# Projecting the gate's two halves in one 512-wide unit at the end of a phase, and reordering the phase

## The chip, the cores and the metric

The kernel runs on one core of a Trainium2 chip. A core has a matrix engine (TensorE, in the profile PE for matmuls and PEld for its weight loads), a vector engine (VectorE, DVE), a scalar engine (ScalarE, ACT), a general engine (GpSimd, POOL) and a queue engine that issues most transfers (SyncE, SP). Each works through its own list of instructions in order and waits on semaphores for the others. Operands lie in SBUF, matmul results in eight PSUM banks of 128 x 512 floats, weights and inputs in HBM. The metric is the device time of one execution in microseconds (us).

## The reference

One layer of a streaming encoder is computed for 1024 prompt rows and 32 sample rows, width 1024, all in float32. What matters here is the first half of the layer:

```python
mod = jax.nn.silu(c) @ w_ada + b_ada
sh1, sc1, g1, sh2, sc2, g2 = jnp.split(mod[:, None, :], 6, axis=-1)
h = x * (1 + sc1) + sh1
mq, mk, mv, mo, mi, mf, fq, fk, fv, ff, gu, gv = jnp.split(h @ w_in, split_at, axis=-1)
hm, (C1, n1, m1) = _mlstm(...)           # 4 heads; mo is its output gate
hf = _fox_prompt(...)                    # 8 heads of causal attention with a decay
vn = _layer_norm(gv, gmlp_ln_g, gmlp_ln_b)
hg = _spatial_gate(gu, vn, gmlp_ws, gmlp_bs)   # gu * (lower-triangular 128x128 mix of vn + bias)
mix = jnp.concatenate([hm, hf, hg], axis=-1) @ w_o
```

A residual, a norm, a SwiGLU feed-forward block of width 2816 and a second norm follow. `gu` and `gv` have 256 columns each; `vn` of the sample rows is an output.

## The kernel before, in words

Every product is done in float32 by parts: an operand x is split into hi (rounded to the matmul's format) and lo = x - hi, and three matmuls (hi·hi, hi·lo, lo·hi) are summed in PSUM. For a weight tile this means a load of 128 x 1024 floats (`raw`), a cast on ACT (`whi`) and a subtraction on DVE or POOL (`wlo`); `weights` does it, with three buffers of each (RAW, WB).

The program has a first phase (0 to some 350 us) and the rest (output projection, norm, feed-forward, to 1345 us). `fm_first` begins it: it makes the modulated input h1 (hi and lo) slice by slice while it projects mq and mk. Two units of 264 columns for the attention's values and gates follow.

A "tm unit" (`tm_unit`) projects rows by columns: for each of eight row tiles of 128 rows it runs 8 x 3 matmuls with the rows as the stationary operand and 256 columns of weights moving, into one of three PSUM banks named g (in the trace tm_g). The ninth tile, the 32 sample rows, uses the unsplit weights (`sample_tile`, 32 small matmuls, L416). An evacuation function then takes each tile out of PSUM.

After that the string ORDER names the units of the phase one by one: q is the projection of one attention head (512 columns, in the trace head_g), f the attention of a head over row tiles 0 to 3 (fox_s scores, fox_p probabilities, fox_t transposes, fox_pth and fox_ptl their split, fox_o the product with the values), g, a, S, s, k are parts of gates, modulation (ada) and states, v and o the mLSTM's values and output gate (tm units, stored to HBM as dmv and dmo), m0 to m3 the mLSTM chunks, which load these again (mlstm_mo), and G0 to G3 the gate's units. A p behind a name puts the weight subtraction on POOL. Units f and m are emitted with a higher priority; a scheduler of the framework turns this into one list per engine, and interleaves units. SP's transfers use eight semaphores in turn, so its list is in order too, and a load that needs an earlier store to land holds up what stands behind it.

The gate takes four tm units of 256 columns: G0 (gv, tiles 0 to 3), G1 (gu, tiles 0 to 3), G2 and G3 (the same for tiles 4 to 8). `evac_gv` reads the PSUM tile for statistics (L472, L473), the reciprocal deviation (L461 to L466, tiles brs and brt) and the normalisation (L477), then POOL multiplies and adds the norm's parameters (L478, L479) and POOL's queue stores the tile in HBM (dvn). `evac_gmlp` copies gu to SBUF, loads the normalised gv of two tiles back (gvn), runs four spatial matmuls for the pair (L848), four gating operations on DVE (L851), transposes (L856), a copy (gms, L858) and a store to dmix, from which the output projection loads its operand. The PSUM bank of the pair's first gu tile is used for the spatial product and the transposes too.

Of the kernel before, what the change touches and what calls it, by code (L numbers as in the profile page):

```python
# [69 lines left out]
class Kernel:  # L70
# [34 lines left out]
    def weights(self, src, nk, ncol, eng=None, pool=None):  # L105

        nc = self.nc
        pool, width = (pool, 1024) if pool else (self.wp, 1056)
        out = []
        step = min(nk, 1056 // ncol)  # L110
        for k0 in range(0, nk, step):
# [1 line left out]
            raw = self.t(self.wp, [P, 1056], F32, "raw", RAW)
# [1 line left out]
            hi = self.t(pool, [P, width], F32R, "whi", WB)
            lo = self.t(pool, [P, width], F32R, "wlo", WB)
            nc.scalar.copy(hi[:, :w], raw[:, :w])  # L117
            (eng or nc.vector).tensor_tensor(lo[:, :w], raw[:, :w], f(hi[:, :w]), ALU.subtract)  # L118
# [348 lines left out]

    def evac_gv(self, tt, ps, n):
        nc = self.nc
        st = self.t(self.sm, [P, 6], F32, "bst", 2)  # L470
        mv = self.t(self.sm, [P, 2], F32, "bmv", 2)
        nc.vector.bn_stats(st[:n], ps[:n, :256])  # L472
        nc.vector.bn_aggr(mv[:n], st[:n])  # L473
        r = self.t(self.sm, [P, 1], F32, "brs", 2)
        self.rstd(r[:n], mv[:n, 1:2], self.eps5[:n], self.sm, "brt")
        v = self.t(self.sm, [P, 256], F32, "traw", 2)
        nc.vector.tensor_scalar(v[:n], ps[:n, :256], mv[:n, 0:1], r[:n], ALU.subtract, ALU.mult)  # L477
        nc.gpsimd.tensor_tensor(v[:n], v[:n], self.rowp[:n, 272:528], ALU.mult)  # L478
        nc.gpsimd.tensor_tensor(v[:n], v[:n], self.rowp[:n, 528:784], ALU.add)  # L479
        self.store(self.dvn[:n, tt, :], v[:n], nc.gpsimd)  # L480
        if tt == 8:
            self.store(self.d["o_vn"], v[:n])
# [346 lines left out]
    def evac_gmlp(self, tt, ps, n, bank=None):  # L829
        nc = self.nc  # L830
        if tt < 8 and tt % 2 == 0:
            self.gu = self.t(self.sm, [P, 2, 256], F32R, "vhl", 2).bitcast(F32)
            self.gbank = ps
        if bank:
            self.gu, self.gbank = ps.unsqueeze(1), bank
        u, z = self.gu, self.gbank
        nt = 1 if tt == 8 else 2
        if tt < 8:
            nc.scalar.copy(u[:n, tt % 2], ps[:n, :256])
        if tt % 2 == 0 and tt < 8:  # L840
            return
        t0 = tt - nt + 1
        vn = self.t(self.sm, [P, 2, 256], F32, "gvn", 1)
        self.load(vn[:n, :nt], self.dvn[:n, t0:tt + 1, :])
        z = z.rearrange("p (t c) -> p t c", t=2)[:n, 2 - nt:]
        for g in range(4):
            q = slice(64 * g, 64 * g + 64)
            nc.tensor.matmul(z[:, :, q], self.wsp[:n, g, :n], vn[:n, :nt, q], start=True, stop=True)  # L848
# [1017 lines left out]
```

## Time and profile before

| | |
|---|---|
| time of 3 runs | 1343.76, 1344.62, 1345.65 us; median 1344.62 |
| span of the profiled execution | 1344.9 us |
| PE busy | 1324.0 us (98%) |
| DVE, ACT, POOL busy | 989.1, 655.8, 231.9 us |
| PE idle in 200 to 250, 250 to 300, 300 to 350 us | 1.1, 0.55, 2.1 us |
| PE idle in 88 to 200 us | 0.0 us |

A row of the timeline gives start, duration, engine, line, operation and "out<-in" with shapes; in square brackets stands the idle time of the engine ahead of it and what ended that. Matmuls are pipelined: a row's duration is longer than the distance to the next start. The view of waits sums such idle times by the waiting line and the line that released it. A row with SPq is the issue of a transfer, not its duration.

### The profile page before, as it was taken

To read this page: it belongs to the slowest core of one execution; us is meant where nothing else is said; L and a number is where in the kernel's file an instruction comes from. 1 tells how busy PE (TensorE), PEld (TensorE's weight loads), DVE (VectorE), ACT (ScalarE), POOL (GpSimd) and SP (SyncE) were. 2 spreads that over 40 slices of the span, in tenths; PEclk is the share of its full clock that TensorE was granted. 3 is DMA by queue.
4 is the path that set the end of the run, shared out by engine and by line. 5 is a ranking of instruction groups with operands and counts; after the bars stand their busy time and mean duration, and the time that the engine had idled before them with its cause. 6 is when DMAs were issued, how large, how long until landed. Compare 5 with 4: busy or idle time off the path is not lost.

```text
span 1344.9 us, 25607 instructions
## 1 busy us (share of the span) xinstructions
PE 1324.0 (98%) x9684; PEld 1208.3 (90%) x9684; DVE 989.1 (74%) x2091; ACT 655.8 (49%) x1305; POOL 231.9 (17%) x263
## 2 busy tenths in 40 slices
PE   9999999999999999999999999999999999999996
PEld 6798888888999888888888888999999999999995
DVE  5635655678779667686876776678979887988777
ACT  3413445455547545545454454435754453635355
POOL 0102100143246100000000001464610000000341
PEclk9999999999999999999999999999999999999999
DMA  9585465546557754454344332663785858554221
GB/s 362 207 299 154 150 204 186 174 131 207 181 195 257 191 136 130 117 163 126 115 121 116 110 104 82 217 175 112 205 231 154 228 148 225 139 175 131 89 79 67
DMA packets 119450, 221.73 MB, mean 165 GB/s; under 512 B 18580, under 2 KB 62768, under 8 KB 119328
## 3 DMA queue, kind: packets, MB, share of 16 engines
q1 hardware_dynamic: 112096, 207.55, 49.0%
q0 software_dynamic: 6032, 11.94, 5.2%
q8 instruction: 76, 1.25, 0.4%
q10 hardware_dynamic: 1200, 0.62, 0.2%
q14 instruction: 46, 0.38, 0.1%
HBM read 188.13 MB, written 51.85 MB: 178 GB/s over the span
## 4 chain that ended last, share of the span: by engine, by line
PE 68%; DVE 4%; DMA 1%; ACT 1%; issue 1%; DVEq 0%; ACTq 0%
PE up_g L130 6%; PE up_g L132 6%; PE up_g L131 6%; PE dn_g L130 4%; PE dn_g L132 4%; PE dn_g L131 4%; PE sup_u L132 3%; PE sup_u L131 3%; PE sup_u L130 3%; PE wo_g L131 2%; PE wo_g L132 2%; PE wo_g L130 2%; PE sup_g L132 2%; PE sup_g L131 2%; PE sup_g L130 2%; PE fox_t L943 2%
## 5 line engine op out<-in xcount | busy, mean ns | idle before, releaser
L130 PE MATMUL up_g<-tm_ah,up_whi 128*128 128x512 f32 (+1 forms) x384 | 140.0, 365 | 0.0
L131 PE MATMUL up_g<-tm_al,up_whi 128*128 128x512 f32 (+1 forms) x384 | 140.0, 365 | 0.0
L132 PE MATMUL up_g<-tm_ah,up_wlo 128*128 128x512 f32 (+1 forms) x384 | 139.7, 364 | 0.0
L1368 ACT CAST sup_whi<-sup_raw 128x1024 fp32r<-128x1024 f32 x54 | 56.1, 1048 | 89.3 <-PE dn_u L131 43.9
L130 PEld LDWEIGHTS up_g<-tm_ah,up_whi 128*128 128x128 f32 x384 | 72.3, 188 | 11.1 <-DVE tm_al L1246 0.4
L132 PEld LDWEIGHTS up_g<-tm_ah,up_wlo 128*128 128x128 f32 x384 | 72.3, 188 | 11.1
L131 PEld LDWEIGHTS up_g<-tm_al,up_whi 128*128 128x128 f32 x384 | 72.3, 188 | 10.7
L916 ACT ACTIVATE fox_p<-fox_s,fox_fmx 128x384 f32<-128x384 f32 (+2 forms) x96 | 55.2, 579 | 53.0 <-DVE fox_fmx L914 41.2
L1199 DVE SCALAR_TENSOR_TENSOR wo_z<-dn_g,start_mod,wo_z 128x512 f32<-128x512 f32 (+4 forms) x120 | 60.3, 521 | 22.6 <-PE dn_g L132 22.0
L118 DVE TENSOR_TENSOR up_wlo<-up_raw,up_whi 128x1024 fp32r<-128x1024 f32 x50 | 65.2, 1305 | 15.0 <-ACT up_whi L117 13.7
L1369 DVE TENSOR_TENSOR sup_wlo<-sup_raw,sup_whi 128x1024 fp32r<-128x1024 f32 x54 | 68.0, 1263 | 10.7 <-ACT sup_whi L1368 10.7
L117 ACT CAST up_whi<-up_raw 128x1024 fp32r<-128x1024 f32 x50 | 52.4, 1048 | 47.2 <-PE up_g L131 23.9
L130 PE MATMUL dn_g<-up_acth,dn_whi 128*128 128x512 f32 (+2 forms) x200 | 73.5, 368 | 0.8 <-DVE wo_z L1199 0.8
L132 PE MATMUL dn_g<-up_acth,dn_wlo 128*128 128x512 f32 (+2 forms) x200 | 73.3, 366 | 0.0
L131 PE MATMUL dn_g<-up_actl,dn_whi 128*128 128x512 f32 (+2 forms) x200 | 72.8, 365 | 0.0
L948 ACT CAST fox_pth<-fox_t 128x512 fp32r<-128x512 f32 (+1 forms) x80 | 41.6, 542 | 59.2 <-PE fox_t L943 57.5
L117 ACT CAST dn_whi<-dn_raw 128x1024 fp32r<-128x1024 f32 (+1 forms) x44 | 42.7, 971 | 51.7 <-PE up_g L131 16.0
L911 DVE TENSOR_REDUCE fox_fmx<-fox_s 128x1 f32<-128x384 f32 (+2 forms) x96 | 52.8, 553 | 16.3 <-PE fox_s L908 15.0
L949 DVE TENSOR_TENSOR fox_ptl<-fox_t,fox_pth 128x512 fp32r<-128x512 f32 (+1 forms) x80 | 49.9, 631 | 15.9 <-ACT fox_pth L948 15.6
L118 DVE TENSOR_TENSOR dn_wlo<-dn_raw,dn_whi 128x1024 fp32r<-128x1024 f32 (+1 forms) x44 | 49.5, 1125 | 10.4 <-ACT dn_whi L117 9.5
L402 PE MATMUL tm_g<-tm_whi,start_h1h 128*128 128x256 f32 (+1 forms) x192 | 55.3, 288 | 0.7 <-DVE tm_traw L477 0.7
L1320 POOL DMA_DIRECT2D start_dp<-w_gu x19 | 19.8, 1067 | 209.0 <-DMA start_dp<-w_gu 209.0
(684 smaller groups left out, 4799.7 us busy)
## 6 DMA issues: line engine op xcount, KB each, us to landing
up_raw<-w_gu SPq DMA_DIRECT2D x50, 512.0 KB
ada_late<-w_ada SPq DMA_DIRECT2D x28, 512.0 KB
dn_raw<-w_dn SPq DMA_DIRECT2D x28, 512.0 KB
sup_raw<-w_gu SPq DMA_DIRECT2D x20, 512.0 KB
start_dp<-w_gu SPq DMA_DIRECT2D x19, 512.0 KB
start_dp<-w_gu POOLq DMA_DIRECT2D x19, 512.0 KB, 8.0
wo_raw<-w_o SPq DMA_DIRECT2D x18, 512.0 KB
sup_raw<-start_dp SPq DMA_DIRECT2D x18, 512.0 KB
```

Of the source, the lines that this page charges most:

```text
L117: nc.scalar.copy(hi[:, :w], raw[:, :w])
L118: (eng or nc.vector).tensor_tensor(lo[:, :w], raw[:, :w], f(hi[:, :w]), ALU.subtract)
L130: nc.tensor.matmul(ps, hi, xh(k), start=start and k == 0, stop=False)
L131: nc.tensor.matmul(ps, hi, xl(k), start=False, stop=False)
L132: self.lastmm = nc.tensor.matmul(ps, lo, xh(k), start=False, stop=stop and k == n - 1)
L402: nc.tensor.matmul(ps[:, :ncol], xh, hi, start=k == 0, stop=False)
L911: nc.vector.tensor_reduce(mxs[:, x:x + 1], s[:, :w], AX.X, ALU.max, negate=True)
L916: nc.scalar.activation(pr[:, lo:hi], banks[x][:, :hi - lo], AF.Exp, bias=mxs[:, 0:1], accum_out=sums[:, x:x + 1])
L949: nc.vector.tensor_tensor(pl[:, :e], ps[:, :e], f(ph[:, :e]), ALU.subtract)
L1199: self.lastz = self.nc.vector.scalar_tensor_tensor(z[:, m, x:y], ps[:, x - a:y - a], g[i], z[:, m, x:y], ALU.mult, ALU.add)
L1368: nc.scalar.copy(h, x)
L1369: tt(l, x, f(h), ALU.subtract)
```

## The change

The four gate units become one: G projects [gv | gu], 512 columns, for all nine tiles, and stands at the end of ORDER, ahead of a last a. The other units are named in a new order; the weight subtractions of G are on DVE. `evac_gv` is gone. `evac_gmlp` now works on pairs of tiles: ACT copies an even tile and then an odd tile whole to SBUF (vhl), DVE takes statistics there, the reciprocal deviation is made once for the pair, DVE normalises each tile in SBUF, POOL multiplies and adds for both tiles at once (128 x 2 x 256), and the spatial matmuls read the result where it stands. The stores to dvn and the loads of gvn are gone. The odd tile's PSUM bank is used for the spatial product and the transposes. `weights` uses tiles of 1024 instead of 1056 columns and four buffers instead of three; the 264-wide units are loaded in 3 + 3 + 2 slices instead of 4 + 4. The first v unit is issued behind the last DVE operation of `fm_first`'s last split. The scratch area of POOL's transfers is 4096 instead of the default.

```diff
-ORDER = "q0 f0 g q1 a f1 a g S q2 f2 k1p s a q3 f3 a v q4 f4 a q5 f5 o a m0 G0 q6 f6 a m1 G1p G2p q7 m2 f7 a m3 G3"
+ORDER = "q0 q1 f0 a g a f1 q2 S k1p g q3 f2 a f3 q4 a v s f4 q5 f5 a q6 o m0 m1 a m2 f6 m3 a q7 f7 G a"
-RAW = 3
+RAW = 4
-WB = 3
+WB = 4
...
-        step = min(nk, 1056 // ncol)
-        for k0 in range(0, nk, step):
+        most = 1024 // ncol
+        for k0 in range(0, nk, most):
+            step = min(most, nk - k0)
...
             self.h1_split(k + 1, h)
+            if k == KT - 2:
+                self.lasth = [i for i in nc.cur_bb.bb.instructions if i.engine == eng.DVE][-1]
...
-        self.tm_unit(w1[0], 264, self.evac_v(0))
+        with tc.issue_after(self.lasth):
+            self.tm_unit(w1[0], 264, self.evac_v(0))
...
-                self.tm_unit(w2[2 + i % 2], 256, (self.evac_gv, self.evac_gmlp)[i % 2],
-                             range(4 * (i // 2), 4 + i // 2 * 5), eng=eng)
+                self.tm_unit(d["w_in_g"], 512, self.evac_gmlp, range(9), eng=eng)
...
-    nc = bacc.Bacc("TRN2", target_bir_lowering=False, num_devices=1)
+    nc = bacc.Bacc("TRN2", target_bir_lowering=False, num_devices=1, dynamic_dma_scratch_size=4096)
```

The evacuation of the gate (the new function up to the spatial matmuls; behind them only the tile names differ):

```python
    def evac_gmlp(self, tt, ps, n, bank=None):
        nc = self.nc
        nt = 1 if tt == 8 else 2
        i, t0 = tt % nt, tt - nt + 1
        if i == 0:
            self.gst = [self.t(self.sm, [P, 2, w], F32, x, 2) for x, w in (("bst", 6), ("bmv", 2), ("brs", 1))]
            self.gx = ps.unsqueeze(1) if bank else f(self.t(self.sm, [P, 1024], F32R, "vhl", 2)).rearrange(
                "p (t c) -> p t c", t=2)
        x, (st, mv, r) = self.gx, self.gst
        if bank is None:
            nc.scalar.copy(x[:, i], ps)
        nc.vector.bn_stats(st[:n, i], x[:n, i, :256])
        nc.vector.bn_aggr(mv[:n, i], st[:n, i])
        if i < nt - 1:
            return
        self.gbank = bank or ps
        vn, u = x[:n, :nt, :256], x[:n, :nt, 256:]
        self.rstd(r[:n, :nt], mv[:n, :nt, 1:2], self.eps5[:n], self.sm, "brt")
        for y in range(nt):
            nc.vector.tensor_scalar(vn[:, y], vn[:, y], mv[:n, y, 0:1], r[:n, y], ALU.subtract, ALU.mult)
        row = lambda o: self.rowp[:n, o:o + 256].unsqueeze(1).to_broadcast([n, nt, 256])
        nc.gpsimd.tensor_tensor(vn, vn, row(272), ALU.mult)
        nc.gpsimd.tensor_tensor(vn, vn, row(528), ALU.add)
        ...
            nc.tensor.matmul(z[:, :, q], self.wsp[:n, g, :n], vn[:, :, q], start=True, stop=True)
```

How the lists of the engines move is shown at three places. First DVE's list at the end of `fm_first`, before: the slice's modulation (ada_h) and its split (start_al, start_h1l) stand behind the subtraction of the first v unit (tm_wlo).

```order
L219 TENSOR_SCALAR start_mod_153<-ada_adam_597,start_colp_108 128x2 x2
L118 TENSOR_TENSOR tm_wlo_680<-tm_raw_677,tm_whi_679 128x1056
L243 TENSOR_SCALAR ada_h_601<-fm_x_529,start_mod_153 128x1024
L244 TENSOR_SCALAR ada_h_601<-fm_x_529,start_mod_153 128x32
L253 TENSOR_TENSOR start_al_170<-ada_h_601,start_ah_169 128x512
L253 TENSOR_TENSOR start_h1l_172<-ada_h_601,start_h1h_171 128x544
```

And now:

```order
L220 TENSOR_SCALAR start_mod_152<-ada_adam_596,start_colp_107 128x2 x2
L244 TENSOR_SCALAR ada_h_600<-fm_x_528,start_mod_152 128x1024
L245 TENSOR_SCALAR ada_h_600<-fm_x_528,start_mod_152 128x32
L254 TENSOR_TENSOR start_al_169<-ada_h_600,start_ah_168 128x512
L254 TENSOR_TENSOR start_h1l_171<-ada_h_600,start_h1h_170 128x544
L119 TENSOR_TENSOR tm_wlo_679<-tm_raw_676,tm_whi_678 128x792
L119 TENSOR_TENSOR tm_wlo_685<-tm_raw_682,tm_whi_684 128x792
```

The subtraction moved behind the whole slice.

Second, ACT's list where the output gate's first tiles (tm_traw) are copied out and chunk m0 takes the gate (mlstm_mo, loaded from HBM) through Exp, Ln, Exp; before:

```order
L452 COPY tm_traw_3037<-tm_g_3012 128x256
L916 ACTIVATE fox_p_2761,fox_fsm_2760<-fox_s_2762,fox_fmx_2759 128x512
L452 COPY tm_traw_3065<-tm_g_3040 128x256
L916 ACTIVATE fox_p_2881,fox_fsm_2880<-fox_s_2882,fox_fmx_2879 128x128
L732 ACTIVATE mlstm_mo_3266<-mlstm_mo_3266 128x256
L948 CAST fox_pth_2776<-fox_t_2771 128x512
L733 ACTIVATE mlstm_mo_3266<-mlstm_mo_3266,start_ones_36_111 128x256
L948 CAST fox_pth_2785<-fox_t_2781 128x384
```

And now:

```order
L455 COPY tm_traw_3098<-tm_g_3073 128x256
L912 ACTIVATE fox_p_2893,fox_fsm_2892<-fox_s_2894,fox_fmx_2891 128x384
L944 CAST fox_pth_2806<-fox_t_2802 128x384
L912 ACTIVATE fox_p_2904,fox_fsm_2903<-fox_s_2905,fox_fmx_2902 128x512
L719 ACTIVATE mlstm_mo_3306<-mlstm_mo_3306 128x256
L720 ACTIVATE mlstm_mo_3306<-mlstm_mo_3306,start_ones_35_110 128x256
L721 ACTIVATE mlstm_mo_3306<-mlstm_mo_3306 128x256
L958 COPY fox_fo_2815<-fox_o_2781 64x512
L455 COPY tm_traw_3126<-tm_g_3101 128x256
L944 CAST fox_pth_2919<-fox_t_2914 128x512
```

The three gate operations stand together now, and the copies of an attention result and of the second tile stand behind them, ahead of the next cast for the attention.

Third, POOL's list at the gate; before, with its own stores and weight subtractions between the norms of single tiles:

```order
L478 TENSOR_TENSOR tm_traw_3422<-tm_traw_3422,start_rowp_176 128x256
L479 TENSOR_TENSOR tm_traw_3422<-tm_traw_3422,start_rowp_176 128x256
L118 TENSOR_TENSOR tm_wlo_3745<-tm_raw_3742,tm_whi_3744 128x1024
L91 DMA start_dvn_63<-tm_traw_3422 128x256
L118 TENSOR_TENSOR tm_wlo_3751<-tm_raw_3748,tm_whi_3750 128x1024
L478 TENSOR_TENSOR tm_traw_3463<-tm_traw_3463,start_rowp_176 128x256
```

And now:

```order
L837 TENSOR_TENSOR tm_vhl_3987<-tm_vhl_3987,start_rowp_175 128x2x256
L722 TENSOR_TENSOR mlstm_mo_3645<-mlstm_mo_3645,start_rowp_175 128x256
L838 TENSOR_TENSOR tm_vhl_3987<-tm_vhl_3987,start_rowp_175 128x2x256
L837 TENSOR_TENSOR tm_vhl_4072<-tm_vhl_4072,start_rowp_175 128x2x256
L838 TENSOR_TENSOR tm_vhl_4072<-tm_vhl_4072,start_rowp_175 128x2x256
```

Stores and weight subtractions are gone from it, and each operation covers a pair of tiles; the multiplication of chunk m3's gate stands between the first pair's two.

More of the change, by code (lines that the diff above doesn't have):

```diff
@@ L107, in weights @@
         nc = self.nc
[L108 removed]
+        pool, bufs = (pool, 3) if pool else (self.wp, WB)
         out = []
[L110 to L111 removed]
+        most = 1024 // ncol
+        for k0 in range(0, nk, most):
+            step = min(most, nk - k0)
             w = step * ncol
[L113 removed]
+            raw = self.t(self.wp, [P, 1024], F32, "raw", RAW)
             self.load(raw[:, :w], src[:, k0 * ncol:k0 * ncol + w])
[L115 to L116 removed]
+            hi = self.t(pool, [P, 1024], F32R, "whi", bufs)
+            lo = self.t(pool, [P, 1024], F32R, "wlo", bufs)
             nc.scalar.copy(hi[:, :w], raw[:, :w])
@@ L310, in split @@
         def split(k):
-            hi, lo = (self.t(self.wp, [P, 1056], F32R, x, WB)[:, :2 * N] for x in ("whi", "wlo"))
+            hi, lo = (self.t(self.wp, [P, 1024], F32R, x, WB)[:, :2 * N] for x in ("whi", "wlo"))
             nc.scalar.copy(hi, raw[k])
@@ L417, in sample_tile @@
                                  start=k == KT - 1, stop=k == 0)
-        r = self.t(self.sm, [NS, 264], F32, "tmsum", 1)[:, :ncol]
+        r = self.t(self.sm, [P, 512], F32, "gms", 1)[:NS][:, :ncol]
         for q in range(4):
             nc.scalar.copy(r[:, n * q:n * q + n], ps[32 * q:32 * q + 32, :n])
-        evac(8, r, NS, *([ps] if evac == self.evac_gmlp else []))
+        evac(8, r, NS, *([ps] if ncol == 512 else []))
     def evac_v(self, half):
@@ L437, in evac @@
             nc.vector.tensor_copy(self.G[:, tt, 8 * half:8 * half + 8], gate)
-            hl = self.t(self.sm, [P, 4, 2, 64], F32R, "vhl", 2)
+            hl = self.t(self.sm, [P, 1024], F32R, "vhl", 2)[:, :512].rearrange("p (h two e) -> p h two e", h=4, two=2)
             src = raw.rearrange("p (h e) -> p h e", h=4)
@@ L447, in evac_raw, with evac @@
         nc = self.nc
-        def evac(tt, ps, n):
+        def evac(tt, ps, n, bank=None):
             if tt < 8:
@@ L466, in rstd @@
         nc.vector.scalar_tensor_tensor(out, v, 1.5, out, ALU.add, ALU.mult)
[L468 to L482, printed above, removed]
     def evac_qk(self, h, act=False):
@@ L830, in evac_gmlp @@
         nc = self.nc
-        if tt < 8 and tt % 2 == 0:
-            self.gu = self.t(self.sm, [P, 2, 256], F32R, "vhl", 2).bitcast(F32)
-            self.gbank = ps
-        if bank:
[L835 to L845, printed above, removed]
+        nt = 1 if tt == 8 else 2
+        i, t0 = tt % nt, tt - nt + 1
+        if i == 0:
+            self.gst = [self.t(self.sm, [P, 2, w], F32, x, 2) for x, w in (("bst", 6), ("bmv", 2), ("brs", 1))]
[7 more added lines that the diff above has]
+        if i < nt - 1:
+            return
+        self.gbank = bank or ps
[6 more added lines that the diff above has]
+        nc.gpsimd.tensor_tensor(vn, vn, row(528), ALU.add)
+        if bank:
+            self.store(self.d["o_vn"], vn[:, 0])
+        z = self.gbank.rearrange("p (t c) -> p t c", t=2)[:n, 2 - nt:]
         for g in range(4):
             q = slice(64 * g, 64 * g + 64)
-            nc.tensor.matmul(z[:, :, q], self.wsp[:n, g, :n], vn[:n, :nt, q], start=True, stop=True)
+            nc.tensor.matmul(z[:, :, q], self.wsp[:n, g, :n], vn[:, :, q], start=True, stop=True)
         for g in range(4):
@@ L856, in evac_gmlp @@
                 nc.tensor.transpose(ps[:, i, x, :n], u[:n, x, i * P:(i + 1) * P], self.ident[:n, :n])
-        s = self.t(self.sm, [P, 2, 2, P], F32, "gms", 1)
+        s = self.t(self.sm, [P, 512], F32, "gms", 1).rearrange("p (i t q) -> p i t q", i=2, t=2)
         nc.scalar.copy(s[:, :, :nt, :n], ps[:, :, :nt, :n])
@@ L1359, in sup @@
         ah, al = act[j] = [self.t(pool, [P, GN[1]], F32R, x, 5) for x in ("acth", "actl")]
-        raw = [self.t(self.wp, [P, 1056], F32, "raw", RAW)[:, :1024] for _ in range(2)]
+        raw = [self.t(self.wp, [P, 1024], F32, "raw", RAW)[:, :1024] for _ in range(2)]
         raw.append(self.t(self.px, [P, 544], F32, "w2", 1)[:, :512])
@@ L1370, in split @@
             return [(h[:, k * P:k * P + P], l[:, k * P:k * P + P]) for k in range(x.shape[1] // P)]
-        big = lambda x: split(*(self.t(self.wp, [P, 1056], F32R, y, WB)[:, :1024] for y in ("whi", "wlo")), x)
+        big = lambda x: split(*(self.t(self.wp, [P, 1024], F32R, y, WB)[:, :1024] for y in ("whi", "wlo")), x)
         w1 = big(raw[0])
@@ L1807, in _layout @@
     a["w_in_1"] = units(np.concatenate([mq, mk[:, :128]], axis=1), 384)[0]
-    a["w_in"] = units(np.concatenate([mv, mo, gv, gu], axis=1), 256)
+    a["w_in"] = units(np.concatenate([mv, mo], axis=1), 256)
+    a["w_in_g"] = units(np.concatenate([gv, gu], axis=1), 512)[0]
     a["w_in_f"] = units(np.concatenate([mk[:, 128:], qk], axis=1), 128)
```

5 lines of the change are left out of this document (2 added, 3 removed).

## The prediction

> **What bounds the kernel now.** I read the page's totals and clock first, then the stretches of time, then what PE waited for, then single rows of the timeline.
>
> ```profile
> span 1344.9 us, 25607 instructions
> PE 1324.0 (98%) x9684; PEld 1208.3 (90%) x9684; DVE 989.1 (74%) x2091; ACT 655.8 (49%) x1305; POOL 231.9 (17%) x263
> PEclk9999999999999999999999999999999999999999
> ```
>
> TensorE (PE) is busy 98% at full clock; the other engines matter only where it waits for them. The view by stretches says where it idles.
>
> ```profile
> core 0: us, PE busy (x) PEld busy (x) DVE busy (x) ACT busy (x) POOL busy (x), PEclk, DMA share, GB/s
> 88.00:200.00 112.00, 112.00 (x907) 99.63 (x907) 63.99 (x206) 46.52 (x111) 11.21 (x18) 1.00 0.58 184
> 200.00:250.00 50.00, 48.90 (x410) 42.77 (x410) 30.15 (x77) 27.90 (x66) 1.37 (x2) 1.00 0.58 177
> 250.00:300.00 50.00, 49.45 (x439) 45.12 (x441) 34.79 (x79) 23.47 (x56) 19.77 (x19) 1.00 0.45 144
> 300.00:350.00 50.00, 47.89 (x437) 43.68 (x426) 42.21 (x125) 26.09 (x69) 13.97 (x20) 1.00 0.58 192
> ```
>
> The change edits 50 to 350 us; there PE idles 1.1 + 0.55 + 2.1 us from 200 on, and nothing from 88 to 200. The waits of PE name the causes:
>
> ```profile
> engine line waited for: us in total, times, longest us
> PE fox_o L951 <- DVE fox_ptl L949: 1.1, 1, 1.1
> PE tm_g L416 <- DVE tm_traw L477: 1.0, 1, 1.0
> PE up_u L132 <- DVE up_wlo L118: 0.8, 1, 0.8
> PE tm_g L416 <- ACT tm_traw L434: 0.7, 1, 0.7
> PE tm_g L402 <- DVE tm_traw L477: 0.7, 1, 0.7
> PE tm_g L402 <- DVE tm_brt L464: 0.6, 1, 0.6
> PE tm_g L848 <- DMA tm_gvn<-start_dvn: 0.4, 1, 0.4
> PE fm_t L329 <- ACT start_hs L254: 0.4, 1, 0.4
> ```
>
> Four of these (L477 twice, L464, the gvn load) belong to the gate's units. All the change can win by removing waits is a few us.
>
> **The change, part by part.**
>
> *Width.* 384 matmuls of 256 columns become 192 of 512. The mean durations suggest much, the starts little:
>
> ```profile
> L402 PE MATMUL tm_g<-tm_whi,start_h1h 128*128 128x256 f32 (+1 forms) x192 | 55.3, 288 | 0.7 <-DVE tm_traw L477 0.7
> 231.33 0.28 PE L404 MATMUL tm_g<-tm_whi,start_al 128*128 128x256 f32 x1
> 232.62 0.28 PE L403 MATMUL tm_g<-tm_wlo,start_ah 128*128 128x256 f32 x1
> 274.68 0.40 PE L132 MATMUL head_g<-start_ah,tm_wlo 128*128 128x512 f32 x1
> 276.08 0.39 PE L132 MATMUL head_g<-start_ah,tm_wlo 128*128 128x512 f32 x1
> ```
>
> Between the first two starts lie 11 steps, 1.29/11 = 0.117 us each; between the last two 6 steps, 1.40/6 = 0.233. Matmuls overlap, so the step is the price: 192 x (2 x 0.1173 - 0.2333) = 0.25 us. I take -0.3 (0 to -1).
>
> *Sample tile.* Two sample tiles of 256 columns (a quarter of them per matmul) become one of 512, 32 matmuls fewer.
>
> ```profile
> 322.72 1.10 PE L416 MATMUL tm_g<-tm_raw,start_hs 128*32 128x64 f32 x64 [1.04 <-DVE tm_traw L477]
> ```
>
> One costs 1.1 us with the switch into it. If columns set its time, only the switch is saved; if the count does, all of one tile. Nearer the first, as the width showed: -0.3 (0 to -1.1).
>
> *Waits of the gate's units.* Their banks were held until DVE's normalisation (L477) had read them; now ACT copies each even tile out and frees it, and the odd tile's bank is kept for the spatial product. The four waits sum to 2.7 us; a matmul's row (0.28) lasts 0.16 longer than its step (0.117), and an idle time counts only from the row's end, so each wait costs 0.16 more: 4 x 0.16 = 0.6. So 3.3 goes (2.7 to 3.4).
>
> The new chain to the spatial product replaces it:
>
> ```profile
> 266.22 0.73 POOL L478 TENSOR_TENSOR tm_traw<-tm_traw,start_rowp 128x256 f32<-128x256 f32 x1 [4.45 <-DVE tm_bmv L473]
> 268.01 0.54 DVE L477 TENSOR_SCALAR tm_traw<-tm_g,tm_bmv,tm_brs 128x256 f32<-128x256 f32 x1
> 263.08 0.43 DVE L472 BATCH_NORM_STATS2 tm_bst<-tm_g 128x6 f32<-128x256 f32 x1
> ```
>
> Per pair: ACT copy 0.6 (estimate, from a 512-wide ACT cast in 234.99 to 235.56 below), statistics 0.6, rstd about 1.2 (two ACT, three DVE steps), two L477-like operations 1.1, two POOL operations twice as wide, so 2 x 1.46 = 2.9: 6.4 us, near 7.5 with hand-overs. By the order PE has 39 matmuls of 512 ahead of the tightest spatial product, 9.1 us, and some attention work. DVE is 84% busy here (42.21 of 50), so it may queue; I charge 0.5 (0 to +2).
>
> That POOL and DVE get in each other's way is to be seen already:
>
> ```profile
> 270.65 2.40 POOL L118 TENSOR_TENSOR tm_wlo<-tm_raw,tm_whi 128x1024 fp32r<-128x1024 f32 x1 [0.40 <-ACT tm_whi L117]
> 270.70 2.36 DVE L464 SCALAR_TENSOR_TENSOR tm_brt<-tm_bmv,start_eps,tm_brs 128x1 f32<-128x1 f32 x1 [1.60 <-ACT tm_brs L462]
> ```
>
> A one-column operation took 2.36 us because POOL began 0.05 earlier. The change drops four such POOL casts and 18 narrow operations (4 x 2.4 + 18 x 0.73 = 22.7 us) for 8 of 1.46 (11.7 us). The Trainium skill, page "SBUF — State Buffer", section "Who interferes with whom", adds a point against the change: a DVE tensor_scalar that stays in SBUF can enter a mode that shares POOL's ports, and the loser waits out the whole instruction; before, L477 read PSUM. By that rule each of the 8 new POOL operations may hold DVE, at most 11.7 us of DVE, less than the 22.7 us that could hold it before; no run here shows that mode yet.
>
> *Start.* The last input slice's operations on DVE now stand ahead of the first weight split of the v unit.
>
> ```profile
> 49.20 1.25 DVE L118 TENSOR_TENSOR tm_wlo<-tm_raw,tm_whi 128x1056 fp32r<-128x1056 f32 x1
> 50.37 0.80 DVE L243 TENSOR_SCALAR ada_h<-fm_x,start_mod 128x1024 f32<-128x1024 f32 x1
> 52.54 0.83 PE L329 MATMUL fm_t<-fm_raw,start_hs 128*32 128x384 f32 x2 [0.39 <-ACT start_hs L254]
> ```
>
> The slice comes 1.17 earlier; PE gets back its 0.4 wait and some of the slack before it: -0.7 (-0.4 to -1.2). The split, now late by some 3 us, is not needed before the v unit's first tile at 59.3.
>
> *Output-gate unit, then mLSTM chunk 0.* In the new order m0 follows o at once. The gate travels through HBM: ACT copies tile 0, SP stores it, SP waits for the landing, loads it back, and ACT, in order, stands still.
>
> ```profile
> 226.71 0.36 ACT L452 COPY tm_traw<-tm_g 128x256 f32<-128x256 f32 x1
> 227.81 0.34 SPq L91 DMA_DIRECT2D start_dmo<-tm_traw  x1
> 232.53 0.34 SPq L87 DMA_DIRECT2D mlstm_mo<-start_dmo  x1
> 234.67 0.42 ACT L732 ACTIVATE mlstm_mo<-mlstm_mo 128x256 f32<-128x256 f32 x1 [4.17 <-DMA mlstm_mo<-start_dmo]
> 234.99 0.57 ACT L948 CAST fox_pth<-fox_t 128x512 fp32r<-128x512 f32 x1
> 352.55 0.46 SPq L91 DMA_DIRECT2D start_dmix<-fox_fo  x1
> 354.86 0.33 SPq L87 DMA_DIRECT2D tm_al<-start_dmix  x1
> ```
>
> Landing took 4.7 us behind queued weight loads, 2.3 at 352.55. In the new order ACT has three mo operations (1.35), a 64x512 copy (0.6), a tile copy (0.36) and the cast (0.57) after the load, DVE the 0.63 split (its group's mean): 3.5 us. From the end of tile 0: 1.5 to the store's issue, 2.3 to 4.7 landing, 2.1 load, 3.5 = 9.4 to 11.8 us. PE has 57 narrow matmuls (6.7) and attention and mLSTM pieces (3.4) ahead of the first piece that needs it: 10.1. Stall 0 to 1.7, against 1.1 + 0.16 now: I take 1.3, no net change (-1.3 to +2.5, as m1's own load queues behind). Also behind that ACT row is the copy of tile 1, which frees a PSUM bank for tile 4; PE gets there later.
>
> *First w_o product.* The last head, f7, now ends inside the next projection. Store to load took 2.3 us (above); with two copies, load and cast about 7.7 us, against 62 matmuls of 272 columns (62 x 0.125, by the same reading of starts) and 15 of 256, 9.5 us: nothing (0 to +2.5, a 4.7 us landing).
>
> *New order elsewhere.* From 88 to 200 no idle time can be won, only caused: +0.7 (0 to +3). *Fourth buffers* let a weight load start one unit earlier; of the 0.8 us that PE waited for up_wlo, late in the program, I credit 0.3 (0 to -1). The two early MB of loads stand before the v unit's third tile, needed some 20 us later: nothing.
>
> Sum: -0.3 - 0.3 - 3.3 + 0.5 - 0.7 + 0 + 0 + 0.7 - 0.3 = **-3.4 us**. The profiled execution's span is 1344.9, the runs' median 1344.62, so 0.3 lower: 1344.6 - 3.4 = **1341.2 us**. All low ends give -8.6, all high ones about +7.
>
> **The rivals.**
>
> *Nothing to be told.* Waits move rather than go: the gate's 3.3 return as queueing at the bank hand-over, on m0 and in the reordered heads. For it: PE idles 3.75 us in the 150 us after 200, and DVE is already 84% busy; against: the removed round trip. Change 0 to -2: 1343.5.
>
> *The clean case.* No new stall, all low ends but half of the rest: -6 us, 1338.6. For it: cover exceeds each chain by 2 us; against: four pairs, m0, f7 and five reordered heads would all have to fit at once.
>
> *Slower: the bank held through the norm.* An odd tile's bank is free only after statistics, POOL, spatial product and transposes; with three banks PE stops once the chain's 7.5 us grow past the 9 to 10 of cover, which DVE's queue and two POOL holds (2 x 1.3) do if each pair meets both. Then each of 4 pairs is late by about 2 us: -3.9 + 8 = +4, 1348.7. Against it: ACT, 52% busy, frees the even banks.
>
> *The wide matmul as the means state it.* 192 x (2 x 0.288 - 0.39) = 36 us: 1309. Against it stand the starts; it would need the 117 ns step to be a limit of something other than columns.
>
> **How the numbers follow.** A change below 0.2% (2.7 us) can't be told from none. Forecast 0.45, nothing 0.25, slower 0.18, clean 0.11, wide 0.01. The forecast's own range is 1339.5 to 1343, four fifths of it below 1341.9: 0.36 faster, 0.09 same. With clean and wide, faster is 0.48; with "nothing" and a slower case that ends short of its price (0.01), same is 0.35; slower is 0.17. The range reaches from the clean case into the slower one: 1337.0 to 1347.5, with a tenth left out on either side.
>
> **What would show it.** Right: no PE wait on L477-like, brt or gvn rows; the step of tm matmuls 0.233; fm_t without a wait at about 51; POOL busy some 10 us less; one PE wait near fox_ptl behind ACT's mo of at most 2 us; 350 to 1345 as before. Wrong: PE waits on vhl (POOL or DVE) or on the gms copy, repeated per pair; an idle PE between 88 and 200; a wait of wo_g on its first operand; or a move of the FFN's stretches.

## The result, and the profile after

The changed kernel runs 1339.53 us at the median, against 1345.13 for the kernel before in the same comparison: a ratio of 0.9948, 95% interval 0.9933 to 0.9964. One of its four executions took 5672.74 us, for no reason that is on record, and counts as slow, so that it is no part of that ratio; the other three took 1338.67 to 1339.63 us. By the medians the change is worth 5.6 us (3.4 were forecast), by the ratio 7.0 (4.8 to 9.0), and the time lies inside the range of 1337.0 to 1347.5. The two profiled executions stand 7.1 us apart. The page of the changed kernel:

```profile
span 1337.8 us, 24992 instructions
PE 1320.8 (99%) x9428; PEld 1198.5 (90%) x9428; DVE 990.1 (74%) x2081; ACT 651.2 (49%) x1291; POOL 212.9 (16%) x242
```

PE is busy 3.2 us less, and the rest of the 7.1 is idle time that has gone: 1344.9 - 1324.0 = 20.9 us of idleness before, 1337.8 - 1320.8 = 17.0 now. What PE still waited for, as the view of its waits has it:

```profile
engine line waited for: us in total, times, longest us
PE wo_g L131 <- DVE wo_z L1195: 2.2, 1, 2.2
PE start_o L295 <- DVE start_onesm L162: 1.2, 1, 1.2
PE ada_t L212 <- ACT ada_adas L207: 0.6, 1, 0.6
PE fox_o L947 <- DVE fox_ptl L945: 0.5, 1, 0.5
```

None of the four waits of the gate's units is left, nor the one at the mLSTM's first chunk, nor the one at the border of the v units, nor that of fm_t. One is new, and the largest: wo_g behind wo_z. Where it lies is seen in the view by stretches (same columns as before; the second column is PE's busy time):

```profile
200.00:250.00 50.00, 50.00 (x420) 42.84 (x419) 33.82 (x88) 31.23 (x76) 1.25 (x2) 1.00 0.55 169
250.00:300.00 50.00, 50.00 (x355) 42.32 (x355) 31.27 (x96) 21.84 (x58) 7.52 (x12) 1.00 0.44 139
300.00:350.00 50.00, 49.91 (x323) 42.82 (x321) 38.69 (x102) 23.04 (x52) 11.85 (x12) 1.00 0.43 141
420.00:950.00 530.00, 527.82 (x3213) 459.35 (x3213) 390.43 (x774) 266.78 (x554) 81.36 (x86) 1.00 0.49 138
950.00:1050.00 100.00, 100.00 (x797) 99.87 (x796) 91.66 (x171) 57.34 (x105) 17.88 (x19) 1.00 0.80 212
```

The last two stretches in the kernel before, and its two waits near 1010 us:

```profile
420.00:950.00 530.00, 529.97 (x3236) 461.87 (x3235) 389.01 (x780) 267.75 (x556) 82.41 (x85) 1.00 0.48 139
950.00:1050.00 100.00, 98.06 (x775) 97.25 (x774) 86.30 (x165) 56.08 (x106) 19.59 (x21) 1.00 0.75 197
PE dn_g L130 <- DVE wo_z L1199: 0.8, 1, 0.8
PE dn_u L130 <- DVE wo_z L1199: 0.4, 1, 0.4
```

From 200 to 350 PE idles 0.09 us instead of 3.75. Behind that, two things happen which were not in the forecast: 2.2 us are lost between 420 and 950, and the 1.9 us that PE idled from 950 to 1050 are gone.

The same is read from when PE reaches a piece of work in both traces. It starts the first tm matmul 0.76 us earlier (58.29 against 57.53), the first w_o product (wo_g) 7.3 us earlier (366.9 against 359.6), its last w_o product only 3.8 us earlier (905.2 against 901.4), the last feed-forward product (up_g) again 7.1 us earlier (1313.1 against 1306.0).

### The profile page after: what moved, and what is told of

It is laid out like the page before. It is cut to its first block, busy times and chain, and to the rows that moved or that the text cites. A ratio compares the mean times of both kernels' runs of the same rounds, so it can differ in the third digit from the quotient of the medians.

```text
span 1337.8 us, 24992 instructions
## 1 busy us (share of the span) xinstructions
PE 1320.8 (99%) x9428; PEld 1198.5 (90%) x9428; DVE 990.1 (74%) x2081; ACT 651.2 (49%) x1291; POOL 212.9 (16%) x242
## 4 chain that ended last, share of the span: by engine, by line
PE 95%; DVE 2%; DMA 2%; ACT 1%; issue 0%; SPq 0%; DVEq 0%
PE up_g L131 6%; PE up_g L133 6%; PE up_g L132 6%; PE dn_g L131 4%; PE dn_g L132 4%; PE dn_g L133 4%; PE tm_g L405 3%; PE tm_g L407 3%; PE tm_g L406 3%; PE sup_u L133 3%; PE sup_u L132 3%; PE sup_u L131 3%; PE fox_t L939 2%; PE wo_g L131 2%; PE wo_g L133 2%; PE wo_g L132 2%
## 5 line engine op out<-in xcount | busy, mean ns | idle before, releaser
L131 PE MATMUL up_g<-ada_ah,up_whi 128*128 128x512 f32 (+1 forms) x384 | 140.8, 367 | 0.0
L132 PE MATMUL up_g<-ada_al,up_whi 128*128 128x512 f32 (+1 forms) x384 | 140.7, 366 | 0.0
L133 PE MATMUL up_g<-ada_ah,up_wlo 128*128 128x512 f32 (+1 forms) x384 | 139.7, 364 | 0.0
L1364 ACT CAST sup_whi<-sup_raw 128x1024 fp32r<-128x1024 f32 x54 | 56.6, 1050 | 97.6 <-PE dn_u L132 41.3
L131 PEld LDWEIGHTS up_g<-ada_ah,up_whi 128*128 128x128 f32 x384 | 72.5, 189 | 11.7 <-issue 0.4
L133 PEld LDWEIGHTS up_g<-ada_ah,up_wlo 128*128 128x128 f32 x384 | 72.6, 189 | 11.2
L132 PEld LDWEIGHTS up_g<-ada_al,up_whi 128*128 128x128 f32 x384 | 72.6, 189 | 10.6
L405 PE MATMUL tm_g<-tm_whi,start_ah 128*128 128x264 f32 (+2 forms) x160 | 49.9, 312 | 0.0
```

The source lines that it names most:

```text
L131: nc.tensor.matmul(ps, hi, xh(k), start=start and k == 0, stop=False)
L132: nc.tensor.matmul(ps, hi, xl(k), start=False, stop=False)
L133: self.lastmm = nc.tensor.matmul(ps, lo, xh(k), start=False, stop=stop and k == n - 1)
L405: nc.tensor.matmul(ps[:, :ncol], xh, hi, start=k == 0, stop=False)
L1364: nc.scalar.copy(h, x)
```

## The experiments

Each edit was made alone where that was possible. The kernel before ran 1345.2 to 1345.5 us at the median beside them, on two chips: e1, e3, e4 and e5 ran on one, all the others on the second. The changed kernel and its variants each spread over 0.7 to 7 us between executions here, so a difference under 1 us is read from the traces only.

Part of that spread is a cost which the view of waits does not show. Behind some waits the clock granted to PE is halved for 3.4 us, in e4 for 6.8. Three stretches of equal length, the changed kernel, e3 and e4 (the number in the first brackets counts PE's matmuls, the third from the end is the granted clock):

```profile
872.00:875.30 3.30, 3.30 (x29) 3.30 (x28) 2.89 (x5) 2.05 (x4) 3.30 (x5) 1.00 1.00 401
874.30:877.60 3.30, 3.30 (x17) 3.30 (x16) 3.20 (x5) 1.76 (x4) 3.30 (x4) 0.50 0.95 379
880.50:883.80 3.30, 3.30 (x15) 3.30 (x16) 2.75 (x7) 2.12 (x4) 1.49 (x2) 0.50 0.74 246
```

In e3 the starts are 0.23 us apart there, and 0.125 just before and behind. One such stretch costs PE 1.7 us (half of 3.4), in e4 2.2, since PE was still waiting in the first part of it. It follows the waits of 1.8 and 2.2 us for wo_z in e2, 1.9 in e3, 2.8 (for mlstm_mhm) in e5, 3.9 in e1 and 6.9 in e4, and in e0 and e2 those for the first loads, at 8 us. It does not follow those of 2.2 in the two executions of the changed kernel and of 2.5 in e8; why, the runs do not show. The kernel before and the changed kernel had none in their profiled executions before the last matmuls, so the result does not hang on it, but the medians of the variants do in part.

**The changed kernel again (e0).**

> The changed kernel itself, beside the experiments on their chip, as the reference for them. Expected: 0.995 of the kernel before, some 1339 to 1341 us, phase 1 7 us shorter and one wait of PE at wo_g behind wo_z of about 2 us, since DVE's weight subtraction (wo_wlo) there takes 5 us instead of 1.4.

1340.32 us, ratio 0.9958 (0.9943 to 0.9972). The first phase was 6.2 us shorter than that of the kernel before; the start cost 1.8 us in two waits for the first loads (0.3 in the other execution). The wait at wo_g is 2.2 us again.

**Width alone (e1).** The wide matmul in two halves.

```diff
+            for c in (slice(0, 256), slice(256, 512)) if ncol == 512 else (slice(0, ncol),):
                 for k in range(KT):
-                nc.tensor.matmul(ps[:, :ncol], xh, hi, start=k == 0, stop=False)
+                    nc.tensor.matmul(ps[:, c], xh, hi[:, c], start=k == 0, stop=False)
...
```

> The changed kernel with one edit: each wide matmul of the gate is issued as two of 256 columns (first all 24 of the left half, then all 24 of the right half, same weights, same bank, same evacuation). 192 matmuls of 512 columns become 384 of 256 again; the norm in SBUF, the order and the buffers stay. Reference: the changed kernel ran 1339.4 us. My theory (the step between starts is the price): +0.3 to +0.6 us, 1339.7 to 1340.0, steps of 0.117 against 0.233. Rival (the mean durations are the price): +36 us, about 1375.

1347.27 us, ratio 1.0009 (0.9997 to 1.002). That is nowhere near the 36 us of the mean durations, but far more than the steps say. The steps are as expected: all tm matmuls of 256 or 512 columns take 94.2 us of PE's time in the changed kernel (of it 3.8 in gaps, where the next start came later than a step) and 96.8 here (5.4 in gaps), so the steps themselves cost 1.0 more. The rest is waits, and 1.7 us of halved clock behind the longest:

```profile
PE wo_g L131 <- DVE wo_z L1196: 3.9, 1, 3.9
PE fm_g L131 <- DVE fm_qkl L480: 1.6, 1, 1.6
PE tm_g L845 <- POOL tm_vhl L839: 0.8, 1, 0.8
```

The scheduler wrote other lists, in which the last pair's norm is late for PE. The width of a matmul is worth 1 us; what comes with another list is worth more.

**Without the rule for the start (e3).**

```diff
-        with tc.issue_after(self.lasth):
-            self.tm_unit(w1[0], 264, self.evac_v(0))
+        self.tm_unit(w1[0], 264, self.evac_v(0))
```

> The changed kernel without the rule that the first v unit is issued behind the last DVE operation of the last input slice. If that rule is what took 0.75 us out of the start: the first tm matmul starts 0.7 us later than in the changed kernel (58.0 instead of 57.3), fm_t waits for start_hs by 0.4 again, and the time is +0.7, about 1340.1. Rival (the smaller weight tiles and earlier loads did it): start unchanged, 1339.4.

1343.04 us, ratio 0.9978 (0.9966 to 0.9989). The first tm matmul starts at 58.38, against 57.53 in the changed kernel (the expectation counts from a zero 0.25 us later), and fm_t waits for start_hs again (0.3 us): the rule gives the 0.8 us. The time is longer by more than the 0.7 expected. In the trace, 3.5 us longer than that of the changed kernel, 1.1 us more are a wait of PE for a load of modulation weights at 431 us, which the edit does not touch, and 1.7 are the halved clock at 874 us.

**The old order with the wide gate at its end (e4).**

```diff
-ORDER = "q0 q1 f0 a g a f1 q2 S k1p g q3 f2 a f3 q4 a v s f4 q5 f5 a q6 o m0 m1 a m2 f6 m3 a q7 f7 G a"
+ORDER = "q0 f0 g q1 a f1 a g S q2 f2 k1p s a q3 f3 a v q4 f4 a q5 f5 o a m0 q6 f6 a m1 q7 m2 f7 a m3 G"
```

> The changed kernel with the units named in the old order, except that the one wide gate unit stands at the end in place of the four. If the gain comes from the gate's unit (waits on its norm gone) and not from the order: within 1 us of the changed kernel, 1338.5 to 1340.5, with the PE wait at the mLSTM chunk 0 (fox_ptl, 1.1 us) back. Rival (the order is what pays): 1342 or more, new PE waits between 100 and 350 us.

1345.74 us, ratio 1.0002 (0.999 to 1.0015): the gain is gone. Not all of it is the order's, as the waits show:

```profile
PE wo_g L131 <- DVE wo_z L1195: 8.2, 2, 6.9
PE ada_t L203 <- DMA ada_late<-w_ada: 0.9, 1, 0.9
PE wo_g L131 <- ACT tm_gms L854: 0.7, 1, 0.7
```

The wait at wo_g, 2.2 in the changed kernel, is 8.2 here: 1.3 at 375 us, and 6.9 at 880 us, 500 us behind the phase that was reordered, with 2.2 of halved clock behind it. This is the longest of e4's ten executions (1350.46 us), so the median has less of both. My theory (the gate alone pays) falls in either case: the first w_o product starts 1.75 us later than in the changed kernel and the feed-forward 4.2 later, both ahead of the long wait.

**The new order with the old gate (e5).** Four units of 256 columns at the end, norm out of PSUM and through HBM, and three raw buffers so that it fits.

```diff
-ORDER = "... q7 f7 G a"
+ORDER = "... q7 f7 G0 G1 G2 G3 a"
-RAW = 4
+RAW = 3
...
-                self.tm_unit(d["w_in_g"], 512, self.evac_gmlp, range(9), eng=eng)
+                self.tm_unit(w2[2 + i % 2], 256, (self.evac_gv, self.evac_gmlp)[i % 2],
+                             range(4 * (i // 2), 4 + i // 2 * 5), eng=eng)
```

> The changed kernel with the gate as before: four units of 256 columns, norm from PSUM, through HBM with POOL's store and a load, one after the other at the end of the new order, weight subtraction on DVE, and three instead of four raw weight buffers so that it fits. Everything else of the change stays. My theory (the gate's waits were 3.3 us, width and sample tile 1.3): 1339.4 + 3 to 5 = 1342.4 to 1344.4, with PE waits on L477-like, brt and gvn rows after 270 us. Rival (order and buffers hold the gain): 1340 or less.

1348.77 us, ratio 1.0026 (1.0016 to 1.0036). That is slower than the kernel before, and above what either theory gave. The first w_o product starts at 369.55, 9.9 us later than in the changed kernel, 1.7 of it by the halved clock behind the longest wait. The waits are spread over the phase:

```profile
PE mlstm_t L824 <- DVE mlstm_mhm L814: 2.8, 1, 2.8
PE fox_o L954 <- DVE fox_ptl L952: 1.0, 2, 0.6
PE fox_s L910 <- ACT fox_p L919: 0.9, 1, 0.9
```

Only two small ones (0.5 and 0.4 us) are at the gate's own rows: DVE and ACT are late for attention and mLSTM work that shares the end of the phase with the gate. The new order does not pay with the old gate. And the wait at wo_g is not there.

**The buffers alone (e2).** The kernel before with the new `weights`, tiles of 1024 columns, the smaller scratch area, and

```diff
-RAW = 3
+RAW = 4
-WB = 3
+WB = 4
```

> The kernel before with the buffers of the change alone: weight tiles of 1024 columns, four raw, whi and wlo buffers, the smaller scratch; gate, order and start as before. If the fourth raw buffer brings the output projection's weight subtraction into POOL's chain of subtractions (the wait of 2 us of the changed kernel): one wo_wlo of 5 us or more around 865 us and a PE wait at wo_g of 2 to 8 us, while the wait for up_wlo (0.8) and the wait at the border of the v units (0.7) go: -1.5 + 2 to 8, 1345 to 1351. Rival (that wait comes from the order or the gate): no such row, about 1343.5.

1348.91 us, ratio 1.0021 (1.0008 to 1.0034): the buffers alone make the kernel slower at the median, as the first theory had it, though two of the ten executions took 1344.8. The waits at up_wlo and at the v border are gone, and two for wo_z have come, at 379 and 881 us, each with the halved clock behind it in this execution, the longest of the ten:

```profile
PE wo_g L131 <- DVE wo_z L1200: 4.0, 2, 2.2
PE tm_g L403 <- DVE tm_traw L478: 1.3, 1, 1.3
871.82 5.03 DVE L119 TENSOR_TENSOR wo_wlo<-wo_raw,wo_whi 128x1024 fp32r<-128x1024 f32 x1
```

That subtraction takes 1.2 to 1.8 us elsewhere. Its neighbours in the kernel before (timeline of DVE and POOL) and in the changed kernel:

```profile
865.19 7.73 POOL L1193 TENSOR_TENSOR wo_z<-wo_z,wo_pv 128x272 f32<-128x272 f32 x7 [17.87 <-ACT wo_pv L1057]
866.62 1.37 DVE L118 TENSOR_TENSOR wo_wlo<-wo_raw,wo_whi 128x1024 fp32r<-128x1024 f32 x1
```

```profile
860.52 5.61 POOL L1189 TENSOR_TENSOR wo_z<-wo_z,wo_pv 128x272 f32<-128x272 f32 x7
862.25 5.03 DVE L119 TENSOR_TENSOR wo_wlo<-wo_raw,wo_whi 128x1024 fp32r<-128x1024 f32 x1
865.64 1.51 POOL L1316 DMA_DIRECT2D start_dp<-w_gu  x1
871.37 0.39 PE L131 MATMUL wo_g<-up_ah,wo_whi 128*128 128x272 f32 x1 [2.19 <-DVE wo_z L1195]
```

In both, POOL subtracts the pivot from seven tiles (L1193, now L1189), and DVE wants to subtract two SBUF tiles beside it. Before, DVE's operation began 1.4 us into POOL's chain and the two took turns: DVE 1.37, POOL 7.73 for its seven. After, it began 1.7 us into the chain and ended only behind the whole of it and a transfer issue, at 867.28; POOL took 5.61. PE then waited 2.19 for a later DVE operation (wo_z), which empties a PSUM bank. In e4 the same operation took 11.06. In e2 only the second wait, at 881 us, follows such a row; ahead of the first no subtraction took over 1.8 us.

**POOL's chain on DVE (e7, and again e11).**

```diff
-        less = lambda: self.nc.gpsimd.tensor_tensor(z[:, m, sl], ...)
+        less = lambda: (self.nc.vector if c else self.nc.gpsimd).tensor_tensor(z[:, m, sl], ...)
```

> The changed kernel with one edit in the second row group's output projection: the subtraction of the pivot (14 operations of 128x272, L1189) is on DVE instead of POOL. If POOL's chain holds DVE's weight subtraction: no wo_wlo above 2 us there, the PE wait of 2.2 us at wo_g is gone, 1337.5 or a little less. Rival (DVE is late for its own load, and more work makes it later): the wait stays or grows, 1340 or more.

1337.42 us, ratio 0.9942 (0.9922 to 0.9963), beside 1340.32 for the changed kernel on the same chip. The edit moves 28 operations, not 14: seven and seven around 860 us, and 14 in a later sum from 1243 us on, which changes no time (from the last w_o product to the last up_g it takes 404.8 us, 404.6 in the changed kernel). DVE has all this more to do, and yet PE does not idle around the place:

```profile
861.98 2.35 DVE L119 TENSOR_TENSOR wo_wlo<-wo_raw,wo_whi 128x1024 fp32r<-128x1024 f32 x2
850.00:890.00 40.00, 40.00 (x319) 39.84 (x318) 31.36 (x62) 15.16 (x30) 14.62 (x13) 1.00 0.70 185
```

Two subtractions took 2.35 us. A later one, at 875 us, still took 3.09, above the 2 that were expected as a limit, and PE did not wait for it. The rival (DVE late for its own load) is out. At the median this version beats both kernels, though its interval overlaps that of e0.

> The changed kernel with the pivot subtraction of the second row group on DVE, once more, as the reference for the three kernels beside it. Expected 1337.4 again (0.994), no wo_wlo above 2 us around 862.

1337.75 us, ratio 0.994 (0.9922 to 0.9958).

**The same edit on the kernel with the buffers alone (e8).**

> The kernel before with the buffers of the change and, in the second row group's output projection, the pivot subtraction on DVE. With the buffers alone it ran 1348.9 (1.0021), with two waits of PE for wo_z of 4.0 us in sum. If POOL's hold on DVE is what the buffers cost: 1348.9 - 4 to 6 = 1343 to 1345, no wo_wlo above 2 us there. Rival (the buffers cost through transfers that collide): 1347 or more.

1344.47 us, ratio 0.9995 (0.9985 to 1.0005), 4.4 us less than e2. The wait at 881 us is gone, so POOL's hold on DVE is part of what the buffers cost. It is not all of it, for the wait in the first row group, whose chain the edit leaves on POOL, is still there, at 378 us; whether POOL is behind that one too was not tried:

```profile
PE wo_g L131 <- DVE wo_z L1200: 2.5, 1, 2.5
```

The two profiled executions stand 6.7 us apart: 1.8 of it at the start of the program, 3.4 in the halved clock behind e2's two waits, and the rest is about the difference of their waits. With the hold at 881 us gone the buffers are worth next to nothing by themselves.

**The same edit with the old order (e9).**

> The changed kernel with the old order of units (the wide gate at the end) and the pivot subtraction on DVE, so that the order is compared free of the wait of 8.2 us which it had at wo_g. If the order itself is worth only the 2 to 4 us by which the first phase and the following stretch were longer: 1337.4 + 2 to 4.5 = 1339.5 to 1342. Rival (the order is worth nothing by itself): within 1 us of 1337.4.

1341.8 us, ratio 0.9972 (0.9961 to 0.9982), 4.05 more than e11. Without the late wait, the order is worth 4 us by the medians; the two profiled executions stand 2.5 apart. The wide gate pays without the order too: beside e8, which has the same buffers and the old gate, e9 is 2.7 us shorter (of it 0.8 is the rule for the start). Its waits, beside those of the start, say where the order matters:

```profile
PE tm_g L405 <- ACT tm_gms L854: 0.9, 1, 0.9
PE wo_g L131 <- ACT tm_gms L854: 0.8, 1, 0.8
PE wo_g L131 <- DVE wo_z L1195: 0.7, 1, 0.7
PE fox_t L939 <- DVE fox_p L920: 0.5, 1, 0.5
```

With m3 named ahead of G, the gate is the last unit, and its own last copies (tm_gms frees the bank of an odd tile) stop PE, twice. In the new order m3 comes earlier and part of a modulation unit stands behind the gate.

**The halves with the same edit (e10).**

> The changed kernel with the gate's wide matmuls in halves and the pivot subtraction on DVE. Its first phase was 4.2 us longer, of which 1.0 was in the steps of the matmuls and the rest in waits behind the last pair (POOL vhl 0.8, DVE fm_qkl 1.6). Expected: 1337.4 + 4 = 1341.5 (1340.5 to 1342.5). Rival (the lock was most of it): 1338 to 1339.

1343.64 us, ratio 0.9991 (0.998 to 1.0001), more than expected. The profiled execution is 3.3 us longer than e11's (1339.4 against 1336.1), in line with the 4 expected; the median is 5.9 above e11's. The other 2.6 us go with the granted clock: the four executions with a mean of 0.997 or more, the profiled one among them, took 1341.5 to 1342.6 us, the six with 0.996 or less 1342.8 to 1346.6. That the halved clock behind a wait is the reason is likely; no trace of a longer execution shows it.

**The kernel before without POOL's weight subtractions (e6).**

```diff
-ORDER = "... m1 G1p G2p q7 m2 f7 a m3 G3"
+ORDER = "... m1 G1 G2 q7 m2 f7 a m3 G3"
```

> The kernel before with the weight subtractions of G1 and G2 on DVE instead of POOL. My reading was that POOL's 2.4 us subtractions held single DVE operations of the norm (2.36 and 2.72 us) and so PE by 0.6 us, while the two waits for L477 come from banks held through the norm. Then: the DVE rows of 2.4 and 2.7 us are gone, the wait for brt (0.6) with them, those for L477 (1.0 and 0.7) stay: -0.7, within what can be told of 1345. Rival (all of the gate's waits come from POOL): -3 us.

1344.29 us, ratio 0.9993 (0.9983 to 1.0002). The one-column operations of 2.36 and 2.72 us are 0.21 and 0.15 here, and the wait for brt is gone. The wait for L477 stays, and the norm stops PE at another place too:

```profile
PE tm_g L402 <- DVE tm_traw L477: 1.5, 1, 1.5
PE mlstm_s L762 <- POOL tm_traw L479: 1.3, 1, 1.3
```

So the gate's waits before seem to be POOL's doing only to a small part; the rest is the norm itself, tile by tile, holding PE (the edit also moves other rows, so this is not settled).

## Why the prediction was right

Direction and range were right; the size of -3.4 us was short of the measured -5.6. The printed terms add up to -3.7, not -3.4 (1340.9 us), and their low ends to -9.0, not -8.6; neither slip changes the reading. By its own steps:

**Width: -0.3, and 0.5 to 1.0 was there.** Steps of 0.233 were seen for the wide matmul (276.60 to 278.46 in the changed trace, eight steps in 1.86 us). Without the gaps, the tm matmuls of 256 and 512 columns take 97.25 - 6.27 = 91.0 us before and 94.2 - 3.8 = 90.4 after; undone alone (e1), 1.0. The reading of mean durations, 36 us, is refuted.

**Sample tile: -0.3, and next to nothing was there.** I put it nearer to columns than to count, which was right, and here it is all columns: 60 of its 64 records take 1.93 us now,

```profile
273.23 1.93 PE L419 MATMUL tm_g<-tm_raw,start_hs 128*32 128x128 f32 x60
```

against 1.10 for all 64 of one half before. Only the wait ahead of the second tile has gone.

**Waits of the gate's units: -3.3 + 0.5, and -3.3 with nothing back was there.** In the trace, PE's starts were late by 0.71, 1.20, 0.85 and 0.62 us at the four places, 3.4 together; in the changed trace, no start there is late by more than a normal change of work. The new chain was short enough. Its pieces, by the view of one line, for DVE's normalisation and POOL's multiplication:

```profile
L835 DVE TENSOR_SCALAR tm_vhl<-tm_vhl,tm_bmv,tm_brs x8: 396/404/447, 293.0 to 343.7; 128x256 f32<-128x256 f32 x8
L837 POOL TENSOR_TENSOR tm_vhl<-tm_vhl,start_rowp x4: 1283/1294/1299, 293.9 to 344.2; 128x512 f32<-128x512 f32 x4
```

POOL's multiplications took 1.29 instead of my 1.46 (its additions 1.29 to 2.14), DVE's operations 0.40 instead of 0.54. The two engines do hold each other: a DVE tensor_scalar in SBUF of 384 columns took 1.16 beside POOL, and 0.41 or 0.42 the other seven times.

```profile
295.82 1.35 POOL L838 TENSOR_TENSOR tm_vhl<-tm_vhl,start_rowp 128x512 f32<-128x512 f32 x1
296.22 1.16 DVE L920 TENSOR_SCALAR fox_p<-fox_p,fox_fsm 128x384 f32<-128x384 f32 x1
```

No such hold reached PE in the gate. POOL is busy 19.0 us less (231.9 to 212.9), where some 10 were forecast; the other 9 were not traced. The slower case (the bank held through the norm) did not come, though e1's 0.8 us at vhl and e9's 1.7 us at gms suggest that it begins as soon as the lists are a little different.

**Start: -0.7, and -0.76 was there** (first tm matmul 58.29, now 57.53), and e3 gives it back.

**Output gate and m0: no net change forecast, -1.3 was there.** The sum for the chain was right in its pieces, and of the two landings the shorter one nearly came:

```profile
232.46 0.37 SPq L91 DMA_DIRECT2D start_dmo<-tm_traw  x1
235.52 0.33 SPq L87 DMA_DIRECT2D mlstm_mo<-start_dmo  x1
237.83 0.42 ACT L719 ACTIVATE mlstm_mo<-mlstm_mo 128x256 f32<-128x256 f32 x1 [1.71 <-DMA mlstm_mo<-start_dmo]
```

Landing 3.1 us, load 2.3. ACT stood 1.7 us, PE not at all. I had taken a value near the upper end of 0 to 1.7; the lower one was right.

**New order elsewhere: +0.7 for stalls from 88 to 200, and none came** (112.00 of 112.00 again). The last head's attention lost 0.7 at 350 (its wait is 0.5); the w_o chain behind f7 had cover, as forecast.

**Fourth buffers: -0.3, and this is the term that was wrong in kind.** I had priced one wait (up_wlo, 0.8), and it is gone; with it went the late starts at 1008 and 1011 us (0.9 and 0.5) and the wait at the border of the v units (0.8, which I had not counted; all of these are gone in e2 too). Against that stand the 2.2 us of wo_g. I had seen POOL hold a DVE operation in the gate and priced it there, and did not ask where else a DVE subtraction that is let go earlier would meet POOL. Neither theory of what e4 would show had the long wait at 880 us, for the same reason. The sign "350 to 1345 as before" failed with this term.

The sum in the first phase is then: width 0.5, gate 3.4, start 0.76, m0 1.3, v border 0.8, less 0.7 at the last head, is 6.1 of the 7.3 us by which wo_g starts earlier; the remaining 1.2 are spread over small changes of work that I did not trace. Behind it, 3.5 us are lost up to the last w_o product (2.4 of them at wo_g, the wait and the 0.16 that a row outlasts its step) and 3.3 are won back up to the last up_g (2.4 of them the three late starts, up_wlo's among them); the rest of both was not traced. That two movements which the forecast did not have cancel is luck: the first phase won twice what was forecast for the whole, and with e4's wait of 6.9 us and its halved clock in place of the 2.2 it would have lost that again (an estimate: 4.7 + 2.2 = 6.9 us more).

## What to carry to other kernels

On an engine that is 98% busy, price a wider instruction by the distance between starts, and look for the gain in the few waits; then ask of every wait that goes what it had kept apart. A change of buffers reaches every later stage that draws on the same pool: read those stages for two engines that hold each other up, and price the worst meeting, not the one that the trace happens to show. When parts of a change act on each other, test the whole with one part undone as well as each part alone: here the buffers alone (e2) and the new order with the old gate (e5) lost, the wide gate in the old order gained nothing (e4) until POOL's chain was out of the way (e9). And before 2 us are put down to an edit, compare the granted clock of the two executions, stretch by stretch.

## What the runs showed of the hardware that was not expected

A DVE operation with two SBUF inputs can be held through a whole chain of POOL operations, not just one: 5.0 us in four kernels with four raw buffers (the changed kernel in both executions, e2 and, with 5.08, e1 and e3) and 11.06 in e4, against 1.37 in the kernel before, where DVE's operation came between two of POOL's. With three raw buffers (before, e5, e6) it was 1.4, in e5 beside the tiles, split buffers and scratch area of the change. The Trainium skill, page "SBUF — State Buffer", sections "SBUF: two separate sides" and "Who interferes with whom", says that such a DVE operation contends with a POOL operation that reads SBUF, and that whoever issues first has the ports for the whole instruction. The traces agree, and add that DVE can be held through several operations in a row. That POOL's next operations go first because they are already in line is my reading: with four buffers POOL's seven rows start 0.73 us apart and last 1.2 to 1.3 each, so they overlap, and in the kernel before the first two start 0.94 apart and last 0.98 and 0.78. Why the fourth raw buffer brings this about is not shown; the runs show only that it does, and that with the chain off POOL no such row took more than 3.85 us (e9) and PE waited for none at that place. It goes the other way round as well. In e7, where the chain is on DVE, a POOL operation that takes 0.8 to 1.7 us elsewhere began in the midst of DVE's operations and took 5.0:

```profile
863.12 5.01 POOL L1067 TENSOR_TENSOR wo_zs<-wo_z 128x272 f32<-128x272 f32 x1
```

The clock granted to PE can be halved for 3.4 us behind a wait of 1.8 us or more (six times past the start in the profiled executions, not behind the 2.2, 2.2 and 2.5 us of three others), and 1.7 us of time go with it that the view of waits does not show.

A tensor_scalar of 256 columns took 0.40 us from SBUF to SBUF and 0.54 from PSUM.
